# A two-layer fp32 trunk: operand splits put ahead of weight preparation, and an even layer finished half by half

## The chip, the cores and the metric

The kernel runs on one core of a Trainium2 chip. The metric is device time in microseconds of one execution. TensorE is PE in the rows, VectorE DVE, ScalarE ACT, GpSimd POOL, SyncE SP.

## The reference

A prompt of 1024 tokens and 8 single sample tokens go through two layers with shared weights, all in fp32. A token has 1024 numbers, the MLP 4096 inner ones. Each layer adds a token mixer and then an MLP to x:

```python
for l in range(DEPTH):
    sh1, s1, g1, sh2, s2, g2 = split(silu(c) @ ada_w[l] + ada_b[l], 6)
    h = rmsnorm(x, norm_mix[l]) * (1 + s1) + sh1
    out = even_mixer(h, ...) if l % 2 == 0 else mamba_mixer(h, ...)
    x = x + g1 * out
    h = rmsnorm(x, norm_mlp[l]) * (1 + s2) + sh2
    x = x + g2 * (square(relu(h @ mlp_w1[l])) @ mlp_w2[l])
y = rmsnorm(x, norm_final)
# end of even_mixer: gated short convolution beside the recurrence's heads o_a
conv = causal_dwconv(cg * hv, sc_buf, sc_w)
out = concatenate([o_a, bg * conv], -1) @ w_out
```

The states of the recurrences and convolutions are outputs too.

## The kernel before

**Numbers.** Every fp32 product is made of three matmuls (mm3): a weight is split into whi and wlo, an operand into a high and a low part, and PE adds whi by high (L501), whi by low (L504) and wlo by high (L505).

**Weights.** They come in units of 128 x 1024 numbers (512 KB). The list of unit_order() fixes their order, and need() and prepare() follow it: when a unit is used, prep() is called for those up to AHEAD = 3 places on. To prepare one means a DMA from SP into raw (two buffers), a cast to whi on ACT (L435, L466 or L476) and a subtraction that gives wlo on DVE (L436, L467 or L477). whi and wlo have three buffers each, so a cast also waits until PE has done with the unit three before.

**Engines.** Each engine works through its own list in order. The scheduler of the language builds these lists from the order in which the program issues the instructions, so a call that stands earlier in the code gets its instructions earlier on each engine.

**Tokens.** Block 0 is 256 tokens, block 1 is 264 (with the 8 samples), block 2 is 512. Blocks 0 and 1 are group 3, the first half; block 2 is group 2.

**The MLPs.** mlp() makes each projection of seven block products with sums of blocks (Strassen-Winograd) in place of eight. The second projection, here the back phase, has 64 units, numbered 0 to 63: eight to each product i from 0 to 5 (unit 27 is i = 3, j = 3), and sixteen half ones to product 6. A full unit is 48 matmuls of 258 columns, 5.74 us. Products 2 to 5 need weights that are sums of two blocks: a second 512 KB is loaded into t, DVE adds or subtracts it (L461, L463, L465), then cast and subtraction follow; sums that are used again go out to memory (sd) and come back. The operands R[i, q] lie in memory (td). load_op() has POOL load one into rr, and split_op() splits it in two halves, each a cast on ACT (L855) and a subtraction on DVE (L856). A finished tile goes into x by L985 and the samples' part by L992. The loop over BOPS in mlp() issues for each unit the matmuls and evacuations, then

```python
prepare(wpos[0] - 1 + AHEAD)
split_op(...)
if j in at and ...: load_op(...)
```

**The even layer's end.** Units ("e", 18) and ("e", 19) give the gates of the last two channel groups: conv_gate() multiplies them in (L1320) and splits the result into ffh and ffl (L705, L706). Units ("eo", 6) and ("eo", 7) are the last rows of the output projection; out_last() adds its tiles into x (L633), and collects squares for the norm (L568, L569, matmul L537). The norm of the MLP is L742, L743, and the split of its result L705 and L706 (hh). The first operand of the MLP is from group 3. Before, both gate units run over blocks 0, 1 and 2, then the outputs over group 3 and group 2.

Of the kernel before, what the change touches and what calls it, by code (L numbers as in the profile page):

```python
# [33 lines left out]
AHEAD = 3  # L34
# [16 lines left out]
def unit_order():  # L51

    o = []
    head = lambda h: (2 if h else 1) * [("e", h), ("e", 4 + h), ("e", 8 + h), ("e", 12 + h)]
    o += head(0) + head(1) + head(2) + [("eo", 0), ("eo", 1)] + head(3)
    o += [("e", 20), ("e", 24), ("e", 21), ("e", 25), ("eo", 2), ("eo", 3), ("e", 16), ("e", 17)]
    o += [("e", 22), ("e", 26), ("e", 23), ("e", 27), ("eo", 4), ("eo", 5), ("e", 18), ("e", 19), ("eo", 6), ("eo", 7)]
    for l in range(2):
        if l == 1:
            o += odd_order()  # L60
        for c in range(NFF // 4):
            o += [(f"w1{l}", 4 * c + j) for j in range(4)] + [(f"w2{l}", 4 * c + j) for j in range(4)]
    return o
# [101 lines left out]
def kernel(ctx: ExitStack, tc: tile.TileContext, A: dict):  # L165
# [502 lines left out]
    def out_last(ws, srcs, res, grps, last, lazy=()):  # L668

        for g in grps:  # L670
            nm = Norm(g) if last(g) else None
            for m in range(KT):
                for b in GRP[g]:
                    out_tile(ws(m), srcs, res, m, b)
                if 1 in GRP[g]:
                    res.fin_sample(m)
                if nm and g not in lazy:
                    nm.add(m)
                if g != 0 or m == 1:
                    bg.tick()  # L680
            if nm:
                gen = last(g)(nm)
                hgen[g] = bg.add(late(nm, gen) if g in lazy else gen)
# [112 lines left out]
    def mlp(l, gi, finish, more=None):  # L796
# [161 lines left out]
        for n, (i, hb, q, mp) in enumerate(BOPS):  # L958
            j = n % 8
            hi, lo = need(f"b{l}", n, AHEAD - 1)  # L960
            if n == 0 and more:
                ada[0] = more()
            elif i == 6 and hb == 0 and j == 0:
                ada_steps(99)
            elif n % 4 == 0:
                ada_steps(1)
            rh, rl = R[i, q]
            seq = BSEQ if i else BFIRST
            qs = [qq for qq, mm in seq if mm == mp]
            for m in (2 * mp, 2 * mp + 1):  # L970
                if q == qs[0]:
                    pts[m] = pd()
                pt = pts[m]
                for b in range(2) if hb is None else (hb,):
                    c = slice(b * hw, b * hw + hw)
                    mm3(pt[:, b, 0:hw], [(hi[:, o:o + P], lo[:, o:o + P], rh[:, k, c], rl[:, k, c])
                                         for k, o in ((k, 256 * k + m % 2 * P) for k in range(4))],
                        q == qs[0], q == qs[-1])
                if q == qs[-1]:
                    for o, th in BOUT[BPROD[i]]:  # L980
                        mt = 4 * o + m
                        gate = mod[:, gi + mt, 0:1]
                        if hb is None:
                            xv = v2(x[:, mt, th * HX:th * HX + HX])
                            V.scalar_tensor_tensor(xv, pt[:, :, 0:hw], gate, xv, op0=ALU.mult, op1=ALU.add)  # L985
                        else:
                            xv = x[:, mt, th * HX + hb * hw:th * HX + hb * hw + hw]
                            V.scalar_tensor_tensor(xv, pt[:, hb, 0:hw], gate, xv, op0=ALU.mult, op1=ALU.add)
                        if hb != 1:
                            sv = pt[:, 0, 0:4] if th else pt[:, 1, hw - 4:hw]  # L990
                            av = acc[:, mt, 4 * th:4 * th + 4]
                            V.tensor_add(av, sv, av)  # L992
            prepare(wpos[0] - 1 + AHEAD)

            split_op(((0, 2, 1, 1, 1, 1, 1, 1), (2, 2, 1, 1, 1, 1, 0, 2), (1, 1, 0, 0, 0, 0, 0, 0))[2 if i == 6 else i][j]
                     if i in (0, 1, 6) else (1, 1, 1, 1, 1, 1, 0, 2)[j])
            at = (4, 5, 6, 7) if i else (2, 3, 6, 7)
            if j in at and i < 6 and i + 1 + at.index(j) // 2 < 7:
                load_op(i + 1 + at.index(j) // 2, (2, 3, 0, 1)[at.index(j)])

            if i == 6 and j == 7 and hb == 0:
                V.tensor_mul(acc, acc, mod[:, gi:gi + KT, 1:9])
                for k in FOURS:
                    V.tensor_add(x[:, k, 512:520], acc[:, k], xs[:, k])
            if i >= 5:
                next(fin, None)
            bg.tick()
# [316 lines left out]
    def even_mixer(res, last, rest):  # L1324
        hgrn_consts()
        V.tensor_scalar(gnh, vec("gn"), -0.5, None, op0=ALU.mult)
        dma(scs, A["st_sc"])
        fa = [new_ff(), new_ff()]
        g01 = head(0, fa[0], rest, fa[1])
        g01 += head(1, fa[1])  # L1330
        fb = [new_ff(), new_ff()]
        g23 = head(2, fb[0])
        bg.drain(*g01)
        out_seq(rows([need("eo", 0), need("eo", 1)]), [ff_src(f) for f in fa], res)
        g23 += head(3, fb[1])
        c0 = conv_uv(0)
        c1 = conv_uv(1)
        bg.drain(*g23)
        ada_steps(99)
        turn = [0]  # L1340

        def alloc(w):
            turn[0] += 1
            return t2(w) if turn[0] % 2 else t3(w)

        def gens():
            yield from ada_gen(0, alloc, ((6, 7, 8, 9), (10, 11)), 2)
            yield from ada_gen(1, alloc, ((0, 1, 2, 3), (4, 5, 6, 7)), 2)
        ada[0], ada_rate[0] = gens(), 0
        cols[1], bg.between = cols[0], ada_between  # L1350
        out_seq(rows([need("eo", 2), need("eo", 3)]), [ff_src(f) for f in fb], res)
        fa = [new_ff(), new_ff()]
        unit_gemm(need("e", 16), (0, 1, 2), conv_gate(c0, fa[0]))
        unit_gemm(need("e", 17), (0, 1, 2), conv_gate(c1, fa[1]))
        c0 = conv_uv(2)
        c1 = conv_uv(3)
        out_seq(rows([need("eo", 4), need("eo", 5)]), [ff_src(f) for f in fa], res)
        fa = [new_ff(), new_ff()]
        u0, u1 = need("e", 18), need("e", 19)
        for b in range(3):  # L1360
            unit_gemm(u0, (b,), conv_gate(c0, fa[0]))
            unit_gemm(u1, (b,), conv_gate(c1, fa[1]))
        bg.width = 1
        bg.between = None
        ws = rows([need("eo", 6), need("eo", 7)])
        ada_steps(99)
        out_last(ws, [ff_src(f) for f in fa], res, (3, 2), last, (2,))
        dma(A["o_scp"], scp_o)
        dma(A["o_scs"], scs)

# [784 lines left out]
```

## Time and profile before

| | |
|---|---|
| median of 3 runs | 2747.32 us (2745.33 to 2750.24) |
| profiled execution | 2746.34 us, span 2744.5 |
| mean granted clock of TensorE | 0.985 |
| PE busy | 2643.4 us, 96% of the span |
| DVE, ACT, POOL busy | 1981.1 (72%), 1484.1 (54%), 266.2 (10%) |
| DMA | 525.63 MB, 192 GB/s over the span |

A granted clock of 1.00 is 2.4 GHz and 0.50 is 1.2 GHz. Times within the span are counted from its start: the even layer's last gates run from 510 to 536, its last outputs to 560, the first MLP's back phase from 900 to 1258, the second's from 2388 to 2733. "Idle before" is the time an engine stood still ahead of an instruction, and the releaser is what ended that. PE busy counts modelled ends of pipelined matmuls, so what it loses at the lower clock does not show as idle time.

### The profile page before, as it was taken

Reading aid. Unit: us, or ns where it says so; the run is one execution under the profiler, and the core shown is the slowest. Engines: PE = TensorE matmul, PEld = TensorE weight load, DVE = VectorE, ACT = ScalarE, POOL = GpSimd, SP = SyncE. Lnnn points to the kernel's source line nnn. Section 1 sums busy time; section 2 is a strip of 40 time slices with the busy share of each in tenths; the row PEclk is TensorE's granted clock in tenths of the full one; section 3 lists DMA queues with packets and bytes.
Section 4 is the critical chain, followed back from the end, with each engine's and each line's share of the span. In section 5 each row is a group of like instructions: output and inputs, shape, how many; then the busy total and the mean of one; then the engine's idle time right before and its main releaser. Section 6 shows DMA issues by size and latency. Waiting matters only on the chain. (4 is left out here: it accounts for less than half of the span.)

```text
span 2744.5 us, 49358 instructions
## 1 busy us (share of the span) xinstructions
PE 2643.4 (96%) x19450; PEld 2436.2 (89%) x19450; DVE 1981.1 (72%) x3668; ACT 1484.1 (54%) x2411; POOL 266.2 (10%) x492
## 2 busy tenths in 40 slices
PE   6999999999999999899999999999999999999898
PEld 4888877889999999899899997787779999999897
DVE  5766542588867576676999988998778776766777
ACT  5785511174455332346887777878756445433234
POOL 0000000012313200000000000000001322310000
PEclk8999999999999999999999999999999999999999
DMA  8232356446648989744554535533335655879765
GB/s 307 66 100 84 97 190 206 139 153 198 228 155 261 387 296 353 255 142 128 161 159 156 185 125 158 146 129 108 120 115 163 228 186 188 290 282 368 269 216 162
DMA packets 191064, 525.63 MB, mean 192 GB/s; under 512 B 24432, under 2 KB 42544, under 8 KB 190832
## 3 DMA queue, kind: packets, MB, share of 16 engines
q1 hardware_dynamic: 142448, 355.25, 40.5%
q0 software_dynamic: 48384, 167.23, 16.6%
q8 instruction: 153, 2.51, 0.4%
q14 instruction: 79, 0.65, 0.1%
HBM read 408.59 MB, written 113.80 MB: 190 GB/s over the span
## 5 line engine op out<-in xcount | busy, mean ns | idle before, releaser
L501 PE MATMUL pg<-hh,whi 128*128 128x256 f32 (+2 forms) x1616 | 534.8, 331 | 7.5 <-ACT hh L603 5.9
L504 PE MATMUL pd<-rr,whi 128*128 128x258 f32 x1792 | 514.9, 287 | 17.2 <-DVE rr L856 17.1
L504 PE MATMUL pg<-hl,whi 128*128 128x256 f32 (+2 forms) x1616 | 522.0, 323 | 1.9 <-DVE hl L604 1.9
L505 PE MATMUL pg<-hh,wlo 128*128 128x256 f32 (+2 forms) x1616 | 521.3, 323 | 0.0
L501 PE MATMUL pd<-rr,whi 128*128 128x258 f32 x1792 | 511.3, 285 | 3.3 <-DVE racc L992 3.3
L505 PE MATMUL pd<-rr,wlo 128*128 128x258 f32 x1792 | 510.1, 285 | 3.6 <-DVE wlo L477 2.9
L476 ACT CAST whi<-raw 128x1024 fp32r<-128x1024 f32 x222 | 231.5, 1044 | 363.0 <-PE pg L504 217.4
L477 DVE TENSOR_TENSOR wlo<-raw,whi 128x1024 fp32r<-128x1024 f32 x222 | 270.8, 1221 | 204.5 <-ACT whi L476 196.9
L504 PEld LDWEIGHTS pd<-rr,whi 128*128 128x128 f32 x1792 | 343.4, 192 | 19.3 <-DVE rr L856 18.8
L501 PEld LDWEIGHTS pd<-rr,whi 128*128 128x128 f32 x1792 | 345.1, 193 | 10.7 <-issue 10.4
L501 PEld LDWEIGHTS pg<-hh,whi 128*128 128x128 f32 x1616 | 306.7, 190 | 50.2 <-issue 17.8
L505 PEld LDWEIGHTS pd<-rr,wlo 128*128 128x128 f32 x1792 | 343.9, 192 | 4.9 <-DVE wlo L477 3.7
L504 PEld LDWEIGHTS pg<-hl,whi 128*128 128x128 f32 x1616 | 306.9, 190 | 30.2 <-issue 4.8
L505 PEld LDWEIGHTS pg<-hh,wlo 128*128 128x128 f32 x1616 | 306.4, 190 | 24.1 <-issue 0.4
L501 PE MATMUL pd<-hh,whi 128*128 128x258 f32 x1024 | 291.8, 285 | 8.1 <-ACT hh L705 4.4
L504 PE MATMUL pd<-hh,whi 128*128 128x258 f32 x1024 | 290.6, 284 | 0.8 <-DVE hh L706 0.8
L505 PE MATMUL pd<-hh,wlo 128*128 128x258 f32 x1024 | 289.2, 283 | 0.0
L466 ACT CAST whi<-t 128x1024 fp32r<-128x1024 f32 x64 | 67.1, 1048 | 253.6 <-PE pd L504 166.6
L501 PEld LDWEIGHTS pd<-hh,whi 128*128 128x128 f32 x1024 | 194.6, 190 | 10.7 <-ACT hh L705 5.1
L504 PEld LDWEIGHTS pd<-hh,whi 128*128 128x128 f32 x1024 | 194.2, 190 | 1.9 <-DVE hh L706 1.4
L505 PEld LDWEIGHTS pd<-hh,wlo 128*128 128x128 f32 x1024 | 194.5, 190 | 0.0
L501 PE MATMUL pg<-ffh,whi 128*128 128x264 f32 (+2 forms) x544 | 177.3, 326 | 0.0
(338 smaller groups left out, 5815.1 us busy)
## 6 DMA issues: line engine op xcount, KB each, us to landing
raw<-W SPq DMA_DIRECT2D x375, 512.0 KB, 4.2
td<-x POOLq DMA_DIRECT2D x224, 258.0 KB, 4.0
rr<-td POOLq DMA_DIRECT2D x112, 516.0 KB, 7.2
t<-ada SPq DMA_DIRECT2D x192, 256.0 KB, 5.4
t<-W SPq DMA_DIRECT2D x32, 512.0 KB, 5.6
sd<-t SPq DMA_DIRECT2D x32, 512.0 KB, 6.2
t<-sd SPq DMA_DIRECT2D x32, 512.0 KB, 5.7
t<-csd SPq DMA_DIRECT2D x64, 256.0 KB, 4.5
```

The costliest lines, as they stand in the source:

```text
L466: S.copy(hi, h)
L476: S.copy(hi, raw)
L477: V.tensor_sub(lo, raw, hi.bitcast(F32))
L501: mm = PE.matmul(pt, wh, xh, start=first and i == 0, stop=False)
L504: PE.matmul(pt, wh, xl, start=False, stop=False)
L505: PE.matmul(pt, wl, xh, start=False, stop=last and i == n - 1)
```

## The change

In mlp() the call of prepare() moves from before split_op() and load_op() to behind them, in both MLPs. At the even layer's end gates and outputs are done for group 3 and then again for group 2, and the four units are listed, loaded and prepared twice. out_last() for group 3 starts with rows 0 and 1 of both blocks; for group 2 it takes four tiles at once, the first source (unit 6) for all four and then the second (unit 7).

```diff
@@ unit_order
-    ... ("eo", 4), ("eo", 5), ("e", 18), ("e", 19), ("eo", 6), ("eo", 7)]
+    ... ("eo", 4), ("eo", 5)]
+    o += 2 * [("e", 18), ("e", 19), ("eo", 6), ("eo", 7)]
@@ out_last
             nm = Norm(g) if last(g) else None
+            n0 = 2 if len(GRP[g]) > 1 else 4
+            done = {}
+            for b in GRP[g]:
+                n = BLK[b][1]
+                pts = [pg() for _ in range(n0)] if len(GRP[g]) == 1 else None
+                if pts:
+                    for m in range(n0):
+                        mm3(pts[m][:, :n], [ws(m)[0] + srcs[0](b)], True, False)
+                for m in range(n0):
+                    if pts:
+                        mm3(pts[m][:, :n], [w + s(b) for w, s in list(zip(ws(m), srcs))[1:]], False, True)
+                        res.add(m, b, pts[m][:, :n])
+                    else:
+                        out_tile(ws(m), srcs, res, m, b)
+                    done[m, b] = True
             for m in range(KT):
                 for b in GRP[g]:
-                    out_tile(ws(m), srcs, res, m, b)
+                    if (m, b) not in done:
+                        out_tile(ws(m), srcs, res, m, b)
@@ mlp, second projection
-            prepare(wpos[0] - 1 + AHEAD)
             split_op(...)
             if j in at and ...:
                 load_op(...)
+            prepare(wpos[0] - 1 + AHEAD)
@@ even_mixer
-        u0, u1 = need("e", 18), need("e", 19)
-        for b in range(3):
-            unit_gemm(u0, (b,), conv_gate(c0, fa[0]))
-            unit_gemm(u1, (b,), conv_gate(c1, fa[1]))
-        bg.width = 1
-        bg.between = None
-        ws = rows([need("eo", 6), need("eo", 7)])
-        ada_steps(99)
-        out_last(ws, [ff_src(f) for f in fa], res, (3, 2), last, (2,))
+        gates = conv_gate(c0, fa[0]), conv_gate(c1, fa[1])
+        srcs = [ff_src(f) for f in fa]
+        for g in (3, 2):
+            us = need("e", 18), need("e", 19)
+            for b in GRP[g]:
+                for u, ev in zip(us, gates):
+                    unit_gemm(u, (b,), ev)
+            if g == 3:
+                bg.width = 1
+                bg.between = None
+            ws = rows([need("eo", 6), need("eo", 7)])
+            if g == 3:
+                ada_steps(99)
+            out_last(ws, srcs, res, (g,), last, (2,))
```

In the listings below each row is an instruction: its line, what it does, what it writes and reads. The changed kernel's lines are higher by 1 (up to the diff's third hunk) or by 18: its L466 and L468 are L465 and L467 of before, L874 is L856, L1003 and L1010 are L985 and L992, L634 is L633, L724 and L760 are L706 and L742.

DVE around unit 35 of the first MLP, before; rr_11244 is that unit's operand, wlo_11446 its weight's low part, and t6_11632 the sum for unit 38:

```order
L465 TENSOR_TENSOR t6_11506<-t6_11506,raw_11508 128x1024
L467 TENSOR_TENSOR wlo_11446<-t6_11447,whi_11445 128x1024
L856 TENSOR_TENSOR rr_11244<-rr_11244 128x1032
L465 TENSOR_TENSOR t6_11565<-t6_11565,raw_11567 128x1024
L465 TENSOR_TENSOR t6_11632<-t6_11632,raw_11634 128x1024
L467 TENSOR_TENSOR wlo_11505<-t6_11506,whi_11504 128x1024
L856 TENSOR_TENSOR rr_11244<-rr_11244 128x1032
```

And now, where rr_11258 is the operand of unit 35, wlo_11472 its weight's low part, and t6_11658 the sum for unit 38:

```order
L874 TENSOR_TENSOR rr_11258<-rr_11258 128x1032
L466 TENSOR_TENSOR t6_11473<-t6_11473,raw_11475 128x1024
L466 TENSOR_TENSOR t6_11532<-t6_11532,raw_11534 128x1024
L468 TENSOR_TENSOR wlo_11472<-t6_11473,whi_11471 128x1024
L874 TENSOR_TENSOR rr_11258<-rr_11258 128x1032
L466 TENSOR_TENSOR t6_11591<-t6_11591,raw_11593 128x1024
L468 TENSOR_TENSOR wlo_11531<-t6_11532,whi_11530 128x1024
L874 TENSOR_TENSOR rr_11319<-rr_11319 128x1032
L466 TENSOR_TENSOR t6_11658<-t6_11658,raw_11660 128x1024
```

The second half of the operand stood behind two more sums and another unit's low part; now it follows its own unit's low part.

DVE ahead of unit 26 of the second MLP, before; t6_27463 is the sum for unit 28, rr_27146 is the operand of unit 26 and wlo_27332 its weight's low part:

```order
L467 TENSOR_TENSOR wlo_27262<-t6_27264,whi_27261 128x1024
L465 TENSOR_TENSOR t6_27463<-t6_27463,raw_27465 128x1024
L985 SCALAR_TENSOR_TENSOR x_25826<-pd_27083,mod_84,x_25826 128x516
L992 TENSOR_TENSOR racc_25842<-pd_27083,racc_25842 128x4
L985 SCALAR_TENSOR_TENSOR x_25827<-pd_27083,mod_84,x_25827 128x516
L992 TENSOR_TENSOR racc_25842<-pd_27083,racc_25842 128x4
L985 SCALAR_TENSOR_TENSOR x_25826<-pd_27108,mod_84,x_25826 128x516
L992 TENSOR_TENSOR racc_25842<-pd_27108,racc_25842 128x4
L985 SCALAR_TENSOR_TENSOR x_25827<-pd_27108,mod_84,x_25827 128x516
L992 TENSOR_TENSOR racc_25842<-pd_27108,racc_25842 128x4
L467 TENSOR_TENSOR wlo_27332<-t6_27334,whi_27331 128x1024
L856 TENSOR_TENSOR rr_27146<-rr_27146 128x1032 x2
```

And now, where rr_27159 is the operand and wlo_27363 the low part; the sum for unit 27 stands just ahead of these rows, that for unit 28 behind them:

```order
L468 TENSOR_TENSOR wlo_27289<-t6_27291,whi_27288 128x1024
L874 TENSOR_TENSOR rr_27159<-rr_27159 128x1032
L1003 SCALAR_TENSOR_TENSOR x_25850<-pd_27107,mod_84,x_25850 128x516
L1010 TENSOR_TENSOR racc_25866<-pd_27107,racc_25866 128x4
L1003 SCALAR_TENSOR_TENSOR x_25851<-pd_27107,mod_84,x_25851 128x516
L1010 TENSOR_TENSOR racc_25866<-pd_27107,racc_25866 128x4
L874 TENSOR_TENSOR rr_27159<-rr_27159 128x1032
L1003 SCALAR_TENSOR_TENSOR x_25850<-pd_27132,mod_84,x_25850 128x516
L1010 TENSOR_TENSOR racc_25866<-pd_27132,racc_25866 128x4
L1003 SCALAR_TENSOR_TENSOR x_25851<-pd_27132,mod_84,x_25851 128x516
L1010 TENSOR_TENSOR racc_25866<-pd_27132,racc_25866 128x4
L468 TENSOR_TENSOR wlo_27363<-t6_27365,whi_27362 128x1024
```

The sum for unit 28 is no longer in front of the evacuations, the operand's halves stand before and among them, and the low part comes last.

DVE at the end of the last outputs, before; pg is a tile of outputs, hh the split operand of the MLP:

```order
L633 SCALAR_TENSOR_TENSOR x_83<-pg_5212,mod_84,x_83 128x512
L737 TENSOR_TENSOR x_82<-x_82,t2_5115 128x4x8
L737 TENSOR_TENSOR x_83<-x_83,t2_5115 128x4x8
L742 SCALAR_TENSOR_TENSOR x_82<-x_82,am_5100,t2_5115 128x512
L738 TENSOR_TENSOR x_82<-x_82,am_5100 128x4x8
L738 TENSOR_TENSOR x_83<-x_83,am_5100 128x4x8
L742 SCALAR_TENSOR_TENSOR x_82<-x_82,am_5100,t2_5115 128x512
L739 TENSOR_TENSOR x_82<-x_82,mod_84 128x4x8
L739 TENSOR_TENSOR x_83<-x_83,mod_84 128x4x8
L742 SCALAR_TENSOR_TENSOR x_82<-x_82,am_5100,t2_5115 128x512 x2
L706 TENSOR_TENSOR hh_5110<-x_82,hh_5109 128x516 x2
```

And now, where pg_5172 to pg_5175 are the second half's first four output tiles:

```order
L760 SCALAR_TENSOR_TENSOR x_82<-x_82,am_5088,t2_5103 128x512
L724 TENSOR_TENSOR hh_5098<-x_82,hh_5097 128x516 x2
L760 SCALAR_TENSOR_TENSOR x_82<-x_82,am_5088,t2_5103 128x512
L724 TENSOR_TENSOR hh_5098<-x_82,hh_5097 128x516
L760 SCALAR_TENSOR_TENSOR x_83<-x_83,am_5088,t2_5103 128x512 x2
L724 TENSOR_TENSOR hh_5098<-x_82,hh_5097 128x516
L634 SCALAR_TENSOR_TENSOR x_82<-pg_5172,mod_84,x_82 128x512
L634 SCALAR_TENSOR_TENSOR x_82<-pg_5173,mod_84,x_82 128x512
L724 TENSOR_TENSOR hh_5098<-x_83,hh_5097 128x516 x2
L634 SCALAR_TENSOR_TENSOR x_82<-pg_5174,mod_84,x_82 128x512
L634 SCALAR_TENSOR_TENSOR x_82<-pg_5175,mod_84,x_82 128x512
```

Before, the last evacuation stood ahead of the first L742; now the evacuations of the second half stand between the norm's instructions of the first half.

## Rows read from the trace of the kernel before

**Rows 1.** Waits of PE, 895 to 1260 us: engine, tile, line, releaser: total us, times, longest.

```profile
PE pd L504 <- DVE rr L856: 7.3, 3, 3.8
PE pd L501 <- DVE racc L992: 3.3, 1, 3.3
PE pd L505 <- DVE wlo L477: 2.9, 2, 2.6
```

**Rows 2.** Waits of PE, 2385 to 2745 us.

```profile
PE pd L504 <- DVE rr L856: 9.8, 4, 4.6
```

**Rows 3.** Timeline of DVE, 1111 to 1122 us: start, duration, [idle before <-releaser].

```profile
1112.37 1.23 DVE L856 TENSOR_TENSOR rr<-rr 128x1032 fp32r<-128x1032 f32 x1
1113.52 1.22 DVE L465 TENSOR_TENSOR t<-t,raw 128x1024 f32<-128x1024 f32 x1
1118.35 1.23 DVE L465 TENSOR_TENSOR t<-t,raw 128x1024 f32<-128x1024 f32 x1 [3.62 <-DMA t<-W]
...
1120.62 1.23 DVE L856 TENSOR_TENSOR rr<-rr 128x1032 fp32r<-128x1032 f32 x1
```

**Rows 4.** Timeline of ACT, 1111 to 1122 us.

```profile
1112.41 1.05 ACT L855 CAST rr<-rr 128x1032 fp32r<-128x1032 f32 x1
```

**Rows 5.** Stretches: length; busy us (instructions) by engine; granted clock; DMA share, GB/s.

```profile
1063.00:1066.00 3.00, 0.68 (x6) 0.47 (x4) 2.90 (x3) 1.56 (x2) 0.00 (x0) 0.99 1.00 295
1066.00:1073.00 7.00, 6.34 (x30) 6.34 (x31) 4.78 (x7) 0.44 (x1) 0.00 (x0) 0.52 1.00 369
1117.00:1121.00 4.00, 1.08 (x10) 0.88 (x8) 2.65 (x3) 2.00 (x2) 0.00 (x0) 0.94 0.41 134
1121.00:1127.40 6.40, 5.50 (x25) 5.50 (x26) 2.98 (x3) 0.00 (x0) 0.00 (x0) 0.50 0.42 149
1235.00:1240.00 5.00, 2.37 (x20) 2.15 (x19) 4.73 (x12) 1.92 (x4) 0.00 (x0) 1.00 0.18 48
2530.00:2540.50 10.50, 8.36 (x68) 7.94 (x66) 6.26 (x10) 4.00 (x4) 0.00 (x0) 1.00 0.94 370
2540.50:2547.00 6.50, 3.92 (x18) 3.92 (x19) 6.50 (x8) 0.00 (x0) 0.00 (x0) 0.50 0.57 211
2596.00:2605.00 9.00, 4.75 (x40) 4.55 (x39) 6.08 (x6) 2.00 (x2) 0.00 (x0) 1.00 0.70 234
2605.00:2609.00 4.00, 4.00 (x23) 4.00 (x22) 1.51 (x2) 0.00 (x0) 0.00 (x0) 0.57 0.37 131
```

**Rows 6.** Timeline of DVE, 2529 to 2544 us.

```profile
2530.13 1.22 DVE L465 TENSOR_TENSOR t<-t,raw 128x1024 f32<-128x1024 f32 x1 [3.96 <-DMA raw<-W]
2531.27 1.22 DVE L467 TENSOR_TENSOR wlo<-t,whi 128x1024 fp32r<-128x1024 f32 x1
2536.60 1.23 DVE L465 TENSOR_TENSOR t<-t,raw 128x1024 f32<-128x1024 f32 x1 [4.11 <-DMA raw<-W]
2537.75 0.75 DVE L985 SCALAR_TENSOR_TENSOR x<-pd,mod,x 128x516 f32<-128x516 f32 x1
...
2541.80 2.37 DVE L856 TENSOR_TENSOR rr<-rr 128x1032 fp32r<-128x1032 f32 x2
```

**Rows 7.** Timeline of ACT, 938 to 960 us.

```profile
938.80 1.05 ACT L855 CAST rr<-rr 128x1032 fp32r<-128x1032 f32 x1 [6.64 <-DMA rr<-td]
```

**Rows 8.** Waits of PE, 500 to 640 us.

```profile
PE pd L501 <- ACT hh L705: 4.4, 1, 4.4
```

**Rows 9.** Stretches at the start of the first MLP.

```profile
560.00:564.25 4.25, 0.01 (x1) 0.01 (x1) 4.25 (x12) 2.96 (x6) 0.00 (x0) 0.99 0.00 0
564.25:571.00 6.75, 5.91 (x22) 5.07 (x23) 6.75 (x12) 6.75 (x13) 0.00 (x0) 0.50 0.00 0
```

**Rows 10.** Groups of DVE, 524 to 571 us: line, shapes, count, busy us, mean ns, idle before.

```profile
L742 DVE SCALAR_TENSOR_TENSOR x<-x,am,t 128x512 f32<-128x512 f32 x8 | 5.7, 747 | 0.0
...
L706 DVE TENSOR_TENSOR hh<-x,hh 128x516 fp32r<-128x516 f32 x6 | 3.9, 690 | 0.0
```

**Rows 11.** Line 855 on ACT, 890 to 1260 us: its idle time, us and times.

```profile
  DMA rr<-td: 6.6, 1
```

More of the change, by code (lines that the diff above doesn't have):

```diff
@@ L56, in unit_order @@
     o += [("e", 20), ("e", 24), ("e", 21), ("e", 25), ("eo", 2), ("eo", 3), ("e", 16), ("e", 17)]
-    o += [("e", 22), ("e", 26), ("e", 23), ("e", 27), ("eo", 4), ("eo", 5), ("e", 18), ("e", 19), ("eo", 6), ("eo", 7)]
+    o += [("e", 22), ("e", 26), ("e", 23), ("e", 27), ("eo", 4), ("eo", 5)]
+    o += 2 * [("e", 18), ("e", 19), ("eo", 6), ("eo", 7)]
     for l in range(2):
```

## The prediction

> **What bounds the kernel now.** I read the page's busy times, then the waits of TensorE stage by stage, then the timelines of DVE and ACT and the granted clock at its longest waits. TensorE works nearly throughout, so only its idle time, and the stretches at its lower clock level, can be won. In the back phases of the two MLPs the waits are for the operand's low part, L856 on DVE: 7.3 us in three waits in the first [rows 1] and 9.8 in four in the second [rows 2]. Beside it the first has 3.3 us on the last step of an evacuation (L992) and 2.9 on a weight's low part (L477) [rows 1].
>
> What L856 itself waits for, DVE's timeline at unit 35 of the first MLP shows [rows 3]: L465, a weight sum for unit 38, stands idle 3.62 us for its transfer, L467 follows, and the operand's second half (L856), which TensorE needs at once, starts only at 1120.62. Its cast had begun on ACT at 1112.41 [rows 4]: ready for 7 us, but queued behind weights that are not urgent. Unit 27 of the first MLP and unit 35 of the second have the same picture. At unit 26 of the second, L465 idles 4.11 us, and four evacuations and an L467 come between it and L856 [rows 6].
>
> Each such wait costs more than itself. After it the granted clock reads 0.50 to 0.57, the 1.2 GHz level, for 4 to 7 us, and there TensorE loses about half of what it is busy [rows 5]:
> - unit 27, first MLP: idle 2.32 + 0.66 = 2.98, and 6.34 us at 0.52 lose 3.04: 6.0 us;
> - unit 35, first MLP: idle 2.92 + 0.90 = 3.82, and 5.50 us at 0.50 lose 2.75: 6.6 us;
> - unit 26, second MLP: idle 2.14 + 2.58 = 4.72, and 3.92 us at 0.50 lose 1.96: 6.7 us;
> - unit 35, second MLP: idle 4.25, and 4.00 us at 0.57 lose 1.7: 6.0 us.
> Together 25.3 us, of which 15.8 idle: nearly all of the 17.1 that L856 is waited for.
>
> **The move of prepare() behind split_op() and load_op().** It adds and removes no instruction. In each back unit the operand's cast on ACT (1.05 us [rows 4]) and its subtraction on DVE (1.23 [rows 3]) pass one weight's cast, sum and low part. POOL's transfers keep their order. In the new DVE order the second half for unit 35 stands right behind that unit's own L467, and unit 38's sum behind both (first listing). The first half held that slot before, at 1112.37 [rows 3], so the second would be done near 1113.6. TensorE asked for it at about 1117.8: of the 4 us from 1117 it was busy 1.08 [rows 5]. So this wait goes, and by the same order those at unit 27 and at unit 35 of the second MLP: 6.6 + 6.0 + 6.0 = 18.6. At unit 26 of the second MLP the sum that idled until 2536.60 no longer stands in front (second listing). The sum at 2530.13 and L467 at 2531.27 [rows 6] are followed by the first half, done near 2533.7, then two evacuations of 0.75 and their short L992, the second half, two more evacuations, and the unit's own L467, done near 2539.2. TensorE got there at about 2538.2 (2.14 us before 2540.5 [rows 5]) and wants the low part in its third matmul, at 2538.5. About 0.7 us of waiting stays, with 0.3 for the L467 before: 5.7 won. Of the three waits of rows 1 the shortest, 7.3 less the two above, some 0.5, goes too. Gross: 18.6 + 5.7 + 0.5 = 24.8.
>
> What is late next is the weight, which now stands behind one or two subtractions of 1.23. For most units this is hidden by the two units (11.5 us, 96 matmuls) by which weights run ahead; low parts are waited for only 2.9 us in the whole first back phase [rows 1]. Where a weight has nothing to spare, one more subtraction costs up to 1.23. I take two such units in the second MLP, 1.6, and 1.15 at unit 40 of the first, where the evacuation that TensorE waits for has one more subtraction ahead of it. On ACT a cast that waits for its transfer now holds a weight that is due sooner. One case is long: the cast at 938.80 idled 6.64 us [rows 7]. Unit 7's weight would be cast behind it, its low part done near 942.3 after that cast and two subtractions, for matmuls that begin near 940.7: 1.5. Sum: 1.6 + 1.15 + 1.5 = 4.3. This part: 24.8 - 4.3 = 20.5 faster. Its bounds: 26 won if all waits on L856 go and nothing is new; a loss in the third rival.
>
> **The even layer's end in two passes.** The matmuls are the same. Added are four weight units: 2 MB on SP's queue (the DMA share is 0.00 from 560 to 571 [rows 9]), four casts of 1.05 on ACT and four subtractions on DVE (1.22 as L467 [rows 6]). What it touches: TensorE waits 4.4 us for the MLP's first operand [rows 8], is idle from 560 to 564.25 and then runs 22 matmuls in 6.75 us at 0.50 [rows 9], which at 0.12 each is 4.1 us too many. The reason is that the norm of the first half starts on DVE only after the last evacuation. Now that half's outputs are done some 12 us before the end, and its norm runs beside the second half. But DVE is the busy engine there, 4.25 of 4.25 us [rows 9], with eight L742 of 0.747 and eight L706 of 0.690 (six of them fall in the stretch of [rows 10]), and the second half's evacuations are now queued between them (third listing). Following the new order by these durations I get these waits of TensorE: 1.35 us for the fourth weight's low part, behind an evacuation; 0.35 at the gates; 3.8 where an output tile needs a bank whose evacuation stands behind L742 and L706; 2.8 before the MLP, for the last evacuation. The MLP would start at full speed at 567.1 on this trace's clock; before it was as if at 568.4 (564.25 + 4.1). If the 3.8 us wait brings the lower clock for the 24 matmuls behind it, the start comes some 3 us later, and half a speed may last into the MLP. So -1.3 to +3.5. I take +0.5: the same DVE work bounds both, which is nearest to no change.
>
> A wait of 2.63 us between 1235 and 1240 left the clock at 1.00, the four longer ones did not [rows 5]. The Trainium skill, TensorE: Matmul & The Clock Gate, section Why this matters for your kernels, tells authors to leave no idle gaps of TensorE between bursts, as the clock drops after one; by that rule the 3.8 us wait speaks against this part, and the sum would be 3 us worse, inside the bound above.
>
> **Sum.** -20.5 + 0.5 = -20.0 on the profiled execution's 2746.34 us (span 2744.5, and 1.8 outside it): 2726. The median of the runs shown is 1.0 higher: 2727. All times below are against that median.
>
> **Rivals.**
> 1. *Transfers set the pace.* Around units 27 and 26 the DMA share reads 0.94 to 1.00 at up to 370 GB/s [rows 5]. If weights arrive at that rate whatever the order, TensorE running ahead meets them later and the waits at these two places come back as waits for sums: 6.0 + 5.7 are lost and -20.0 becomes -8.3: 2739. Against it: at unit 35 the share is 0.41 [rows 5], and the sum that idled there, done at 1119.6 [rows 3], is for a unit that starts after 1140. The Trainium skill, DMA: Bandwidth & Descriptors, section Where 436 GB/s comes from, puts the HBM side of one core near 358 GB/s; by that rule these stretches are full, which favours this rival, and the trace's 370 agrees.
> 2. *The waits change their name.* If eight of the 128 units have nothing to spare, at 1.5 each, and one of these waits lowers the clock for 3 us, 15 us come back and 5 stay won: 2742. For it: weights are prepared in the same two queues; against it: the 2.9 us above.
> 3. *Slower.* The operand's cast goes ahead of the weight's on ACT. If its transfer is as late as in rows 7 in each of products 1 to 5, every weight behind it waits too: ten places in two MLPs at 6.64 less the 3 us that a weight is usually early, 36 us against 25 won: +11, 2758. It decides from the point where a transfer lands later than the first cast's new turn, some 5 us sooner. Against it: in the first back phase a cast idled for its transfer only once [rows 11].
> 4. *The seam wins as well:* the half-by-half order returns the wait of rows 8 and the slow matmuls behind it, 6 us more: 2721.
>
> **Chances.** Forecast 0.58, rival 1 0.15, rival 2 0.10, rival 3 0.08, rival 4 0.09. A change is told from none at about 0.2%, 5.5 us. Faster are the forecast, rivals 1 and 4 and part of rival 2, less a little for what a new order does unforeseen: 0.79; same 0.12; slower 0.09. The range goes from below rival 4 to past rival 2: 2717 to 2745; the forecast's own is 2720 to 2733.
>
> **What would show it.** In the profile after, TensorE's waits for L856 fall from 17.1 us to under 4, the lower clock is gone behind units 27 and 35, and the waits for low parts (L467, L477) rise by 3 to 5 us. The seam from the even layer to the MLP moves by less than 4 us. The prediction is wrong if the waits for L856 stay, if waits for weights take over 8 us, or if the seam costs or gives more.

## The result and the profile after

The changed kernel takes 2726.70 us, median of 4 runs (2724.08 to 2731.98), against 2748.56 for the kernel before (4 runs, 2745.33 to 2750.24): ratio 0.9925, 95% interval 0.9910 to 0.9939. The forecast was 2727. A repetition on another chip gave 0.9943 (0.9924 to 0.9961). The profiled execution of after is the slowest of its four runs: 2731.98 us, span 2730.2, granted clock 0.988 (0.985 before). The two spans differ by 14.3 us, and only these 14.3 can be looked for in the two traces.

The page of after first, its costliest groups with operand rr, the products of the back phases (line, engine, operation, count, then busy us, mean ns, and after the second bar idle time before them with its main releaser):

```profile
L502 PE MATMUL pd<-rr,whi 128*128 128x258 f32 x1792 | 509.6, 284 | 10.5 <-DVE racc L1010 10.5
L506 PE MATMUL pd<-rr,wlo 128*128 128x258 f32 x1792 | 507.8, 284 | 7.9 <-DVE wlo L468 6.4
L505 PE MATMUL pd<-rr,whi 128*128 128x258 f32 x1792 | 511.4, 285 | 0.0
```

L505 multiplies by the operand's low part, and is never late now: its 0.0 stands where L856 had cost 17.1 us [rows 1, 2]. But two other waits have grown. TensorE's waits by stage, first back phase, 895 to 1260 us (total us, times, longest):

```profile
PE pd L502 <- DVE racc L1010: 10.5, 4, 6.5
...
PE pd L506 <- DVE wlo L478: 1.3, 1, 1.3
```

and second back phase, 2365 to 2745 us:

```profile
PE pd L506 <- DVE wlo L468: 6.4, 4, 2.9
```

L1010 is the last step of an evacuation, 3.3 us before (L992, [rows 1]) and 10.5 now. Low parts of weights, 2.9 [rows 1] and 0.6 in the second phase before, are 7.7 now. The four old places themselves are clean. Stretches of after (length; busy us by PE, PEld, DVE, ACT, POOL; granted clock; DMA share; GB/s):

```profile
1059.00:1073.00 14.00, 14.00 (x117) 13.02 (x117) 9.89 (x9) 6.81 (x8) 0.00 (x0) 1.00 0.93 321
1073.00:1076.00 3.00, 0.41 (x5) 0.23 (x3) 3.00 (x8) 0.47 (x1) 0.00 (x0) 0.93 1.01 326
1076.00:1080.00 4.00, 4.00 (x22) 4.00 (x23) 4.00 (x8) 0.00 (x0) 0.00 (x0) 0.63 0.54 217
1117.00:1127.40 10.40, 10.40 (x87) 9.42 (x86) 7.74 (x14) 4.91 (x7) 0.00 (x0) 1.00 0.74 251
1149.00:1156.00 7.00, 0.51 (x5) 0.30 (x3) 5.08 (x8) 0.36 (x2) 0.00 (x0) 0.86 0.64 220
1156.00:1161.00 5.00, 4.96 (x23) 4.99 (x24) 5.00 (x9) 3.96 (x5) 0.00 (x0) 0.51 0.21 79
2530.00:2547.00 17.00, 17.00 (x144) 17.00 (x143) 14.63 (x17) 6.01 (x6) 0.00 (x0) 1.00 0.91 330
2573.00:2577.00 4.00, 1.09 (x9) 0.88 (x9) 3.05 (x5) 2.00 (x2) 0.00 (x0) 1.00 0.17 46
2577.00:2582.00 5.00, 5.00 (x31) 5.00 (x31) 5.00 (x13) 0.00 (x0) 0.00 (x0) 0.66 0.54 178
2596.00:2609.00 13.00, 13.00 (x110) 13.00 (x110) 10.61 (x16) 6.00 (x7) 2.10 (x4) 1.00 0.76 256
```

Units 27 and 35 of the first MLP (1059 to 1073, 1117 to 1127) and 26 and 35 of the second (2530, 2596) now run without a gap at the full level. In their place there are gaps at unit 28 (1073 to 1076), at unit 40 (1149 to 1156) and, in the second MLP, at unit 33 (2573 to 2577), each again followed by a stretch at 0.51 to 0.66.

With the clock's loss counted as the prediction counted it, the account of the first back phase is this. Before: 6.0 and 6.6 at the two units, 0.5 for the small wait, 2.9 for low parts, and 4.9 at unit 40 (3.31 idle at 1160, then 4.64 us of work at 0.66, below): 20.9. After: unit 40 6.54 + 4.96 x 0.49 = 9.0, unit 28 2.59 + 4.0 x 0.37 = 4.1, shorter waits for L1010 1.4, low parts 1.3: 15.8. That is 5.1 less; from the first matmul of this stage to its last the traces show 357.2 us before and 352.6 after, 4.6 less. Second back phase: 6.7 + 6.0 + 0.8 for the rest of L856 + 0.6 = 14.1 before, 6.4 + 1.7 (5.0 us at 0.66) = 8.1 after: 6.0 less, and by the traces 345.0 against 337.8, 7.2 less. So the move won some 11.8 us in these two profiles. The rest of the 14.3 lies in stages of which the change touches nothing or only the seam.

The prediction had missed that unit 40 already lost clock. A stretch of the kernel before:

```profile
1160.00:1165.00 5.00, 4.64 (x26) 4.67 (x27) 4.37 (x9) 4.19 (x6) 0.00 (x0) 0.66 0.42 156
```

DVE's timeline of after shows unit 35's second half in its new place (start, duration, idle before and its releaser in brackets):

```profile
1112.53 1.23 DVE L466 TENSOR_TENSOR t<-t,raw 128x1024 f32<-128x1024 f32 x1 [0.24 <-DMA raw<-W]
1113.67 1.22 DVE L468 TENSOR_TENSOR wlo<-t,whi 128x1024 fp32r<-128x1024 f32 x1
1114.80 1.23 DVE L874 TENSOR_TENSOR rr<-rr 128x1032 fp32r<-128x1032 f32 x1
1115.95 1.23 DVE L466 TENSOR_TENSOR t<-t,raw 128x1024 f32<-128x1024 f32 x1
1119.83 1.22 DVE L466 TENSOR_TENSOR t<-t,raw 128x1024 f32<-128x1024 f32 x1 [2.66 <-DMA t<-W]
```

L874 is done at 1116.0, and the sum that waits for its transfer (2.66 us) stands behind it. The same view 37 us later shows what became the longest wait:

```profile
1150.92 1.23 DVE L464 TENSOR_TENSOR t<-raw,t 128x1024 f32<-128x1024 f32 x1 [7.44 <-DMA t<-sd]
1152.07 1.23 DVE L874 TENSOR_TENSOR rr<-rr 128x1032 fp32r<-128x1032 f32 x1
1153.21 1.22 DVE L468 TENSOR_TENSOR wlo<-t,whi 128x1024 fp32r<-128x1024 f32 x1
1154.34 0.75 DVE L1003 SCALAR_TENSOR_TENSOR x<-pd,mod,x 128x516 f32<-128x516 f32 x1
...
1155.74 0.15 DVE L1010 TENSOR_TENSOR racc<-pd,racc 128x4 f32<-128x4 f32 x1
```

and TensorE's:

```profile
1156.04 0.55 PE L502 MATMUL pd<-rr,whi 128*128 128x258 f32 x1 [6.54 <-DVE racc L1010]
```

A sum idles 7.44 us for its second block. Behind it stand an operand's half, a low part and the two pairs of L1003 and L1010 that free the bank which unit 40 needs: the second L1010, at 1155.74, lets TensorE go on at 1156.04, after 6.54 us. It is the old picture with another instruction behind the blocked one.

This sum was blocked before the change too. The same place in the kernel before, DVE and TensorE:

```profile
1156.39 1.22 DVE L463 TENSOR_TENSOR t<-raw,t 128x1024 f32<-128x1024 f32 x1 [6.69 <-DMA t<-sd]
...
1160.06 0.15 DVE L992 TENSOR_TENSOR racc<-pd,racc 128x4 f32<-128x4 f32 x1
```

```profile
1160.36 0.36 PE L501 MATMUL pd<-rr,whi 128*128 128x258 f32 x1 [3.31 <-DVE racc L992]
```

TensorE now gets there 7.5 us earlier (it begins to wait near 1149.5, before near 1157.0), but the sum starts only 5.5 us earlier. These 2.1 us and the subtraction that now stands in between (L874, 1.14) are the 3.2 us by which the wait grew. Unit 28 shows the first of the two alone: TensorE asks for its bank at 1073.4, where before it asked at 1078.5 and did not wait, while the sum ahead of that evacuation starts 1.3 us later than before (1070.12 against 1068.83).

At the seam, waits from 500 to 640 us:

```profile
PE pd L502 <- ACT whi L442: 4.4, 1, 4.4
PE pg L502 <- DVE x L634: 3.6, 1, 3.6
PE pd L502 <- DVE x L634: 1.3, 1, 1.3
```

and two stretches there:

```profile
560.50:564.00 3.50, 3.49 (x9) 2.81 (x10) 3.50 (x6) 0.48 (x1) 0.00 (x0) 0.56 0.00 0
564.00:569.00 5.00, 3.75 (x17) 2.67 (x15) 5.00 (x9) 3.47 (x5) 0.00 (x0) 1.00 0.00 0
```

The first wait was there before too. The 4.4 us for hh [rows 8] is gone, and an output tile now waits 3.6 for a bank and the MLP 1.3 for the last evacuation. The lower level (0.56) falls on the last outputs instead of on the MLP's first matmuls [rows 9]. The MLP begins at 569.0 at full speed, where before it began at 564.2 at half; its back phase begins at 899.7 against 900.4.

### The profile page after: what moved, and what is told of

It reads as the page before. It is cut to its first block, busy times and chain, and to the rows that moved or that the text cites. A ratio compares the mean times of both kernels' runs of the same rounds, so it can differ in the third digit from the quotient of the medians.

```text
span 2730.2 us, 49367 instructions
## 1 busy us (share of the span) xinstructions
PE 2637.2 (97%) x19450; PEld 2429.4 (89%) x19450; DVE 1984.6 (73%) x3672; ACT 1488.4 (55%) x2415; POOL 266.2 (10%) x492
## 4 chain that ended last, share of the span: by engine, by line
PE 57%; DVE 15%; DMA 14%; issue 7%; ACT 5%; POOL 2%; SPq 1%; DVEq 0%; POOLq 0%; ACTq 0%
PE pd L502 8%; PE pg L502 8%; PE pd L505 8%; PE pd L506 8%; PE pg L505 8%; PE pg L506 8%; DMA raw<-W 6%; DVE wlo L478 2%; PE psm L324 1%; DMA t<-sd 1%; POOL td L231 1%; DMA t<-W 1%; ACT whi L477 1%; DMA t<-csd 1%; DMA t<-st_ss 1%
## 5 line engine op out<-in xcount | busy, mean ns | idle before, releaser
L505 PE MATMUL pg<-hl,whi 128*128 128x256 f32 (+2 forms) x1616 | 523.0, 324 | 1.9 <-DVE hl L605 1.9
L502 PE MATMUL pd<-rr,whi 128*128 128x258 f32 x1792 | 509.6, 284 | 10.5 <-DVE racc L1010 10.5
L505 PE MATMUL pd<-rr,whi 128*128 128x258 f32 x1792 | 511.4, 285 | 0.0
L505 PEld LDWEIGHTS pd<-rr,whi 128*128 128x128 f32 x1792 | 340.9, 190 | 0.5 <-issue 0.5
L505 PEld LDWEIGHTS pg<-hl,whi 128*128 128x128 f32 x1616 | 307.4, 190 | 30.5 <-issue 5.1
L505 PE MATMUL pd<-hh,whi 128*128 128x258 f32 x1024 | 289.2, 283 | 0.0
L505 PEld LDWEIGHTS pd<-hh,whi 128*128 128x128 f32 x1024 | 193.1, 189 | 0.5 <-issue 0.5
L467 ACT CAST whi<-t 128x1024 fp32r<-128x1024 f32 x64 | 67.1, 1048 | 215.7 <-PE pd L505 122.6
```

The lines of the kernel that those rows point to most:

```text
L467: S.copy(hi, h)
L502: mm = PE.matmul(pt, wh, xh, start=first and i == 0, stop=False)
L505: PE.matmul(pt, wh, xl, start=False, stop=False)
```

## The experiments

Theory (called queue theory in the expectations): DVE works its list in order, and an urgent half stood behind a sum that waits for a transfer; the move takes it out from behind, and the rest of the change does nothing. Rivals: the new seam gives part of the gain, and the transfers set the pace, so that the wait only changes its name. Ratios are against the kernel before on the same chip (medians of it: 2746.80 for e1 to e4, 2757.61 for e5 to e8, 2745.23 for e9 to e12); times of different chips are not compared.

| run | us | ratio (95%) |
|---|---|---|
| e1, only the move | 2728.69 | 0.9934 (0.9920 to 0.9948) |
| e2, only the even layer's end | 2747.36 | 1.0003 (0.9990 to 1.0015) |
| e3, after, DVE's sums and evacuations in program order | 2730.79 | 0.9949 (0.9932 to 0.9965) |
| e4, after without second loads | 2709.15 | 0.9866 (0.9850 to 0.9882) |
| e5, before without second loads | 2724.70 | 0.9892 (0.9871 to 0.9914) |
| e6, after, stores of sums on POOL | 2768.57 | 1.0047 (1.0029 to 1.0066) |
| e7, move in the second MLP | 2750.81 | 0.9982 (0.9967 to 0.9997) |
| e8, move in the first MLP | 2752.54 | 0.9985 (0.9971 to 0.9999) |
| e9, after again | 2730.82 | 0.9943 (0.9924 to 0.9961) |
| e10, as e7 | 2738.24 | 0.9973 (0.9961 to 0.9986) |
| e11, as e8 | 2739.16 | 0.9978 (0.9968 to 0.9988) |
| e12, after, sums on POOL | 2790.84 | 1.0164 (1.0144 to 1.0184) |

**e1 and e2: one part alone.** e1 is before with only the third hunk of the diff, e2 is before with all but that.

```diff
e1 (on before)
-            prepare(wpos[0] - 1 + AHEAD)
             split_op(...)
             if j in at and ...:
                 load_op(...)
+            prepare(wpos[0] - 1 + AHEAD)
e2 (on after): the same lines the other way round
```

> Only the move of prepare() behind the operand's splits, the even layer's end as before. Queue theory (the operand's low part stood behind weight sums that waited for transfers; the even layer's end is neutral): ratio to before 0.991 to 0.995 as for the whole change, waits of TensorE for L856 gone (17.1 us to under 1), and the seam before the first MLP as before, a 4.4 us wait for hh. Rival (the even layer's end carries a good part, since the stretch from the MLP's start to its back phase became 5.5 us shorter in the profile): ratio 0.996 or more.

> Only the even layer's end in two passes, prepare() where it was. Queue theory: ratio 0.998 to 1.002; the back phase of the first MLP begins within 2 us of before (900.4) in the profile, since a start 4.8 us later is given back by the matmuls that no longer run at 0.50; waits for L856 stay near 17 us. Rival (the seam carries a part): ratio 0.997 or less.

e1 keeps nearly the whole gain, e2 none. In e1 there is no wait for the operand's low part, and the new ones are there; its waits from 895 to 1260:

```profile
PE pd L501 <- DVE racc L992: 9.7, 4, 5.5
...
PE pd L505 <- DVE wlo L477: 2.0, 2, 1.0
```

In e2 the old wait stays (7.3 us in the first back phase and 9.3 in the second); its waits from 895 to 1260:

```profile
PE pd L505 <- DVE rr L874: 7.3, 2, 3.9
PE pd L502 <- DVE racc L1010: 3.2, 1, 3.2
```

The seam of e1 is as before (4.4 us for hh), and e2's first back phase begins at 899.9, before at 900.4, both as expected. The gain belongs to the move, and the even layer's end is neutral within 0.15%.

**e3: can order alone remove the new wait?** Sums and evacuations are held to their program order on DVE, so that no sum stands ahead of an evacuation that the program issues earlier.

```diff
-  V.tensor_sub(h, h, raw)                       # and the other two sums
+  tc.keep_in_program_order(V.tensor_sub(h, h, raw))
-  V.scalar_tensor_tensor(xv, ...)               # both evacuations into x
+  tc.keep_in_program_order(V.scalar_tensor_tensor(xv, ...))
-  V.tensor_add(av, sv, av)
+  tc.keep_in_program_order(V.tensor_add(av, sv, av))
```

> The changed kernel, with the weight sums (L461 to L465 of before) and the evacuations (L985, L988, L992) of the second projection kept in program order on DVE, so that no sum that waits for a transfer stands ahead of an evacuation. If the new waits for L992 (10.5 us in four waits) come from that queue, they go, with 1.5 and 2.4 us of lower clock behind the two long ones: 10 to 14 us below the changed kernel, about 2714; waits for low parts (6.4 us) stay. Rival (transfers set the pace, waits only change their name): within 4 us of the changed kernel, with waits for whi or wlo up by as much as those for L992 fall.

No gain: 2730.79 against 2728.69 of the move alone on the same chip. The long waits at units 28 and 40 are gone, and low parts are waited for 1.7 us in place of 7.7. But there are 2.9 us for whi, and at unit 24 TensorE waits 10.1 us for L1010, until 1057.00, so that L1010 costs 11.5 in all. DVE's timeline there:

```profile
1040.35 1.23 DVE L466 TENSOR_TENSOR t<-t,raw 128x1024 f32<-128x1024 f32 x1 [7.70 <-DMA raw<-W]
...
1050.61 1.22 DVE L466 TENSOR_TENSOR t<-t,raw 128x1024 f32<-128x1024 f32 x1 [6.62 <-DMA raw<-W]
...
1056.71 0.15 DVE L1010 TENSOR_TENSOR racc<-pd,racc 128x4 f32<-128x4 f32 x1
```

and its stretches:

```profile
1030.00:1046.00 16.00, 15.40 (x127) 14.22 (x126) 4.82 (x4) 2.25 (x3) 3.15 (x6) 1.00 1.00 376
1046.00:1057.00 11.00, 0.94 (x8) 0.77 (x8) 5.20 (x8) 2.95 (x3) 0.00 (x0) 0.77 0.89 325
```

Two sums idle 7.70 and 6.62 us for a block of theirs, in a stretch where the DMA share is 1.00 at 376 GB/s: there it is the transfers that are late. The theory's expectation of this run failed. The rival's time held (within 4 us), but not its trade: waits for L1010 did not fall, and those for low parts did. And the second of these sums still stands ahead of the evacuation that TensorE waits for: the program prepares weights up to three units ahead, so a sum can come first in program order too. This run moved the blocked sum and did not take it out of the way, so it does not tell order and transfers apart.

**e4 and e5: one of a sum's two loads taken out.** A sum is made of raw and raw; 64 loads of 512 KB per execution go, the DVE work stays. The weights of products 2 to 5 are then not those of the reference, and where the sum is a subtraction they are zero. Whether that alone changes the granted clock was not tried, so the reading rests on the waits more than on the times.

```diff
             h = t6()[:, 0:1024]
-            dma(h, a)
             raw = load_unit(*second)
-                V.tensor_sub(h, h, raw)         # and the other two sums
+                V.tensor_sub(h, raw, raw)
```

> The changed kernel without the second load of each of the 64 weight sums; the sum is taken of the first load alone, so 64 transfers of 512 KB are left out. Queue theory: sums no longer block DVE, so the waits for L992 and for the low parts of summed weights (17 us together) nearly vanish, and with the clock behind them the time is 18 to 24 us below the changed kernel, 2703 to 2709. Rival (these waits are work of DVE and ACT itself, 2.3 us per unit, not transfers): within 5 us of the changed kernel.

> The kernel before without the second load of each of the 64 weight sums (the sum is taken of the first load alone), prepare() still ahead of the splits. Queue theory (what stood in front of the operand's low part was a sum that waited for transfers): waits for L856 fall from 17.1 us to under 3 and the time is within 4 us of the changed kernel without these loads, 2705 to 2713. Rival (the weight's own cast, sum and low part in front of the split suffice, 3 to 4 us of work per unit): waits for L856 of 8 us or more stay, and the time is 2716 or more.

Waits of e4 from 895 to 1265; in the second back phase neither rr, racc nor wlo is in its list:

```profile
PE pd L505 <- DVE wlo L477: 1.2, 2, 1.0
PE pd L501 <- DVE racc L1009: 1.1, 1, 1.1
```

Waits of e5, which keeps the old order, from 895 to 1265:

```profile
PE pd L504 <- DVE wlo L476: 2.6, 1, 2.6
PE pd L503 <- DVE rr L855: 0.5, 1, 0.5
```

and from 2380 to 2760:

```profile
PE pd L503 <- DVE rr L855: 2.4, 5, 1.0
```

With the loads gone, the old order's wait for the operand falls from 17.1 to 2.9 us, and the new order's waits for L1010 from 10.5 to 1.1. Both had the same cause, a sum that blocks DVE while its transfer is on the way. Without that cause the two kernels are 0.26% apart (0.9866 and 0.9892, on two chips, intervals that overlap) where they had been 0.57 to 0.75%. e5's time itself was expected 12 to 20 us lower; its chip ran the kernel before 11 us slower than the others, and in ratio 0.985 to 0.988 had been expected. By its time alone the rival's condition (2716 or more) is met, by its waits (8 us or more) it is not.

**e6: the stores of sums to another queue.** SP's queue carries weights, stores and reloads of sums; the stores go to POOL's.

```diff
             _, d, h = sums.pop(0)
-            dma(d, h)
+            dma_aux(d, h)
```

> The changed kernel with the 32 stores of weight sums (sd<-t) issued by POOL in place of SP, where each waits for its sum ahead of the next loads. If SP's queue makes the sums late, the waits that are left in the back phases (9 us for L992, 6 for low parts) halve: 5 to 10 us below the changed kernel, 2717 to 2722. Rival (the transfers themselves and the two raw buffers set the pace): within 3 us of the changed kernel, waits for L992 and low parts 12 us or more. Against both: operand loads that queue behind a store on POOL, then ACT waits for rr and the time is above 2730.

Slower than the kernel before by 0.47%, and so some 1% slower than the changed kernel (0.9925 and 0.9943). That is the side of the third case, but not by the path which it named: waits for rr are 0.6. From 895 to 1265:

```profile
PE pd L502 <- DVE racc L1010: 16.7, 5, 6.3
PE pd L502 <- ACT whi L467: 6.3, 3, 3.3
PE pd L506 <- DVE wlo L468: 3.2, 5, 0.9
PE pd L505 <- DVE rr L874: 0.6, 2, 0.3
```

The same kind of wait grew. A store took 8.7 us from issue to landing there and 7.0 on SP in after; whether later stores, and so later reloads, explain the rise was not tried.

**e7, e8, e9, e10, e11: where in the program.** Each half of the move alone, and the whole again.

```diff
+            if l == 1:                # e7, e10: second MLP; e8, e11: l == 0
                 prepare(wpos[0] - 1 + AHEAD)        # behind load_op
```

> The kernel before with prepare() moved in the second MLP alone. Queue theory, both MLPs give their part: ratio 0.9955 to 0.9975, 7 to 12 us, the first MLP's back phase with its 7 us of waits for L856, the second with none. Rival (the gain comes from one place): ratio 0.999 or more, or the whole 0.9934.

> The kernel before with prepare() moved in the first MLP alone. Queue theory: ratio 0.9955 to 0.998, 5 to 12 us, since 7 us of waits for L856 and 5.8 us of lower clock go and some 7 us of waits for L992 come; with the second MLP's part it adds up to the 18 us of both. Rival as for the second MLP alone: 0.999 or more, or the whole.

> The changed kernel once more, beside the two halves of its move on one chip. Both theories: ratio 0.991 to 0.995.

> The move in the second MLP alone, beside the whole change on one chip. If the halves add up: it and the first MLP's half together give the whole within 0.15%, some 0.33% each (on the other chip 0.18% and 0.15%). Rival (the gain of one half is lost where the other is missing, or the chip decides): the two together stay under two thirds of the whole.

> The move in the first MLP alone, beside the whole change on one chip. As for the second MLP alone: with it the whole within 0.15% if the halves add up; under two thirds of the whole together otherwise.

e7 and e8 gave less than was expected (0.9982 and 0.9985), and their intervals end just below 1, so they were repeated beside the whole. There the halves give 0.27% and 0.22%, together 0.49%, against 0.57% for the whole: they add up, within the intervals. Each half removes its own wait and leaves the other: e10 has 6.9 us for L856 in the first MLP and none in the second, e11 none and 8.2.

**e12: the sums off DVE's list.** The 64 sums go to POOL, so that a blocked sum has nothing urgent behind it.

```diff
-                V.tensor_sub(h, h, raw)         # and the other two sums
+                nc.gpsimd.tensor_sub(h, h, raw)
```

> The changed kernel with the 64 weight sums (L461 to L465 of before) on POOL in place of DVE, so that a sum that waits for its transfers blocks no evacuation and no low part. Queue theory: the 17 us of waits for L992 and low parts that the change left go down to under 6, with the lower clock behind them: 8 to 16 us below the changed kernel of the same call. Rival (the transfers set the pace): waits move to whi or wlo, within 3 us of the changed kernel. Against both: POOL's sum takes over 4 us, or the operand's loads behind it come late, and it is slower than the changed kernel.

Slower than the kernel before by 1.64%, and than the changed kernel on the same chip (e9) by 2.2%. Groups of POOL and DVE from 900 to 1280 in e12:

```profile
L466 POOL TENSOR_TENSOR t<-t,raw 128x1024 f32<-128x1024 f32 x16 | 42.8, 2675 | 56.5 <-DMA t<-W 21.1 <-DMA raw<-W 17.9 <-DMA t<-sd 15.2
L874 DVE TENSOR_TENSOR rr<-rr 128x1032 fp32r<-128x1032 f32 x52 | 80.6, 1555 | 38.8 <-ACT rr L873 38.7
L468 DVE TENSOR_TENSOR wlo<-t,whi 128x1024 fp32r<-128x1024 f32 x32 | 47.0, 1469 | 64.0 <-ACT whi L467 56.3 <-PE pd L506 7.5
```

A sum takes 2.68 us on POOL, where DVE needed 1.23, and DVE's own subtractions grow from 1.23 us ([rows 3]; 1230 and 1222 ns in this stage of after) to 1.56 and 1.47. Sums come later, and so all that hangs on them: TensorE waits 27.1 us for L1010 in the first back phase and 24.2 for whi in the second. Of the two causes that the expectation named for a slower kernel, the sum of over 4 us did not come, but late operand loads did: ACT idles 44.6 us for them in the first back phase, in after 25.6. How much of the loss is due to each was not told apart. No version that keeps the weights of the reference was measurably faster than the changed kernel.

## Why the prediction was right, and where not

**The mechanism was right.** A sum that waits for its transfer blocked the operand's half behind it on DVE. The move took the 17.1 us of [rows 1, 2] to nothing, the lower clock went from the four places of [rows 5], e1 shows that the move alone does it, and e5 that the blocked sum was the cause: the old order with one of each sum's two loads gone waits 2.9. The place forecast for unit 35's second half, done near 1113.6, was 1116.0 in the trace, still ahead of the request.

**The seam was right in size.** Forecast +0.5 (-1.3 to +3.5); e2 measures +0.03% (-0.10 to +0.15), that is +0.8 us (-2.7 to +4.1). The forecast waits of 3.8 and 2.8 are there with 3.6 and 1.3, and those of 1.35 and 0.35 are not. The lower clock came behind the 3.6, as the bound said, and so the MLP starts at 569.0, not 567.1. As e2's interval leaves no room for 6 us won, the fourth rival is out.

**The failing step is the sum of what is late next: 4.3 us was forecast.** By the account above, 26.6 us went with the waits for L856, and 15.5 came anew:
- unit 40 of the first MLP: forecast 1.15; it cost 9.0 where 4.9 had been, 4.1 more. The one more subtraction ahead of the evacuation, which the prediction counted, cost what it said (1.14). It overlooked that ahead of that stands a blocked sum (idle 6.69 us before, 7.44 after) whose transfer does not come earlier by as much as TensorE does, 2.1 us more, that the wait had its own lower clock before (0.66) and that a longer one would make it 0.51.
- unit 28 of the first MLP: not forecast; 4.1, and shorter waits for L1010 1.4.
- two units of the second MLP: forecast 1.6; low parts are waited for 6.4 us in four waits, with 1.7 more at the lower clock, 7.5 more than the 0.6 of before. Not all of that is the move's: the old order has 4.8, 4.6 and 2.6 us there in e2, e8 and e11, the new one 6.2 to 8.4 (e1, e7, e9, e10).
- unit 7 of the first MLP: forecast 1.5; no such wait. A cast there idles 12.90 us on ACT for its operand's transfer, against 6.64 [rows 7], and its line's idle time there is 25.6 us against 6.6 [rows 11], but no wait of TensorE for L874 follows. So the third rival's mechanism occurs, and TensorE loses nothing by it. Low parts in the whole stage cost 1.6 less than before.

So by the profiles the back phases give 11.8 us, not 20.5. Of the marks the prediction set, L856 (under 4), the clock at units 27 and 35 and the seam (under 4) came true, and waits for low parts took 7.7, just under the 8 at which it called itself wrong. Their rise of 4.2 lies in the 3 to 5 that it forecast, but by luck: 1.6 less in the first MLP and 5.8 more in the second make it up. It had no mark for evacuations, which grew most.

**The time was right beyond what the profiles explain, and in part by luck.** The forecast's -20.0 stands beside -21.9, -18.1 (e1) and -14.4 (e9) in medians, and -14.3 between the two profiled spans. The account explains about 11.8 of these, and the other profiles say the same. From its first matmul to its last the first back phase took 353.5 to 358.8 us in four profiles with the old order in it (before, e2, e7, e10) and 349.7 to 352.6 in five with the new (after, e1, e8, e9, e11); the second took 345.0 to 351.8 (before, e2, e8, e11) and 337.3 to 343.7 (after, e1, e7, e9, e10). By the means that is 4.1 and 8.3 less, 12.4 together. What lies between the two back phases, which the change does not touch, took 1125.2 us in e1 and 1130.6 in e2 on one chip, so some 5 us of a difference between two profiles can be variation. With its largest loss mis-sized by 11 us, the prediction's hit to 0.3 us is not owed to its sum alone. Whether the rest of the medians' gain is variation between executions (after's four runs span 7.9 us) or small gains elsewhere stays open.

**The first two rivals were wrong as wholes and right about the rest.** Waits did change their name, and by the account more than half of the gross gain went back (15.5 of 26.6 us), but not the time of 2739 or 2742. TensorE running ahead meets transfers later at units 28 and 40, as the first rival had it. e3 has late transfers in one full stretch, and e4 shows that what remains hangs on the sums' loads: without half of these another 20 us go (2709.15 against 2728.69 of e1).

## What to carry to other kernels

In an engine's in-order list, put short work that another engine needs now ahead of work that may still wait for a transfer; in the timeline look for an idle instruction with an urgent one behind it. Then price what stands behind the blocked instruction in the new order, by the blocked time itself and not only by the length of one more instruction: ask how much earlier TensorE will come, and whether the transfer comes earlier too. Add the lower clock that follows. Here a third order (e3) only moved the wait, and fewer bytes (e4) removed it; earlier loads were not tried.

## What the runs showed of the hardware

**DVE is slower beside POOL.** An fp32 sum of 128 x 1024 takes 2.68 us on POOL and 1.23 on DVE, and beside it DVE's subtraction L874 goes from 1.23 to 1.56 us on average. In e12's trace the 26 of them that overlap a sum on POOL take 2.24 us on average and up to 3.43, the 86 others 1.24 at most; L1003, which reads one of its two large inputs from TensorE's output bank, takes 0.74 in both cases. The Trainium skill, SBUF — State Buffer, section Who interferes with whom, says that a DVE instruction with two inputs in SBUF contends with a GpSimd instruction that reads SBUF; e12 agrees.

**Transfers went faster than the prediction allowed.** A stretch of after:

```profile
920.00:940.00 20.00, 20.00 (x169) 20.00 (x168) 5.51 (x5) 6.07 (x7) 6.32 (x12) 1.00 1.03 412
```

That is 412 GB/s for 20 us on a core that runs alone. The Trainium skill, DMA: Bandwidth & Descriptors, section Where 436 GB/s comes from, which the prediction cited, has some 358 for the HBM side of one core, and the prediction saw 370 agree with it [rows 5]. This row does not agree, and it decides; the 370 that seemed to agree lay above 358 already. Shares of 1.00 and more go with 295 [rows 5] to 412 GB/s, so one rate does not tell when the transfers are at their limit.

**A gap costs more than itself, but not each does.** In after, idle times of 2.59, 2.91 and 6.54 us were followed by 0.63, 0.66 and 0.51 over 4 to 5 us, a further 1.5 to 2.4 us each; the 2.63 us of the kernel before [rows 5] left 1.00.
